# Four resident sums and four turning PSUM banks in place of five and three

## The chip, the cores and the metric

The kernel runs on one core of one Trainium2 chip. The metric is the device time of one execution in microseconds. The kernel before was timed in 3 runs: median 3021.09 us, from 3012.32 to 3032.1 us.

## What is computed

One decoder layer over 1024 tokens of width 1024: a mixing layer (gated linear recurrence and short convolution), then a retrieval layer over 16384 single-neuron experts, then a final norm. Cut to the part that the change touches:

```python
def peer(h, w_query, sub_keys, expert_u, expert_v):
    def block(xb):
        ...                                   # top-k over two lists of 128 keys, 8 heads, 16 picks each
        gate = jax.nn.softmax(best_s, axis=-1)
        u = expert_u[idx]
        v = expert_v[idx]
        act = jax.nn.gelu(jnp.einsum('td,thkd->thk', xb, u).astype(jnp.float32), approximate=False)
        return jnp.einsum('thk,thkd->td', (gate * act).astype(xb.dtype), v)
...
x = x + gate2 * PEER(h)
return rmsnorm(x, final_norm_w)
```

## The kernel before

The 1024 tokens are split. For 672 of them (the dense tokens, columns 0 to 671, in two pieces of 384 and 288 columns, `SPL`) the retrieval is done as two dense matrix products over all 16384 experts, with the gates as a mostly empty matrix. For the other 352 tokens the picked rows of `expert_u` and `expert_v` are fetched by indirect DMA and multiplied on VectorE: this is the background work. It is laid between the dense work by a budget (`along` and `advance`): so many columns of dense products let so many background steps be issued. A background step is one row fetch on GpSimd's queue into one of five row buffers (four named `grow_`, one named `more`, L1084), then either a product with a sum (L1102) or a multiply-add into `gacc` (L1094), both 128x1024 on VectorE.

The last stage, of which the change is a part, runs over 128 blocks of 128 experts. For a block:

- `u_steps` (L1163): the expert rows `uT` times the normed tokens, 24 products of 384 columns into one PSUM bank `pa` and 24 of 288 columns into the next. ScalarE reads each bank with a gelu (L1168). For 40 of the blocks (every third one, as long as they last) this was done in earlier stages, and the result is loaded from DRAM (`ged`).
- `w_step`: times the gates on VectorE (L1384), then a split into a high and a low part: ScalarE copies the high part (L115), VectorE subtracts (L116).
- `v_load`: 128 rows of `expert_v`, split in the same way. The weights `uT` are split so too (`wh`, `wl`).

After every third block `v_phase` (L1403) multiplies three blocks of `v` with the three gated activations. The output has 16 pieces, (j, c): j is one of the two column pieces, c one of 8 groups of 128 features. Each piece takes 9 products here, three blocks by three split terms, into one PSUM bank. From here on a call of `v_phase` is called a v part, and the products of L1163 between two of them a u part. A piece takes one of two ways:

- A fixed piece (listed in `FIXED`) has a PSUM bank of its own (`pacc`), in which all 128 blocks are summed. It is read once, at the end, by ScalarE (L1411).
- Any other piece is a turning piece. It takes a bank from `new_pv` for its 9 products, and VectorE adds it to an accumulator `acc` in SBUF (L1419), which frees the bank. In the first v part this is a copy (L1417), in the last a multiply-add (L1413) on an accumulator that was scaled before (L1487).

PSUM has eight banks: five for the fixed pieces, one `pv`, and two `pa`, which the u parts use as well. `new_pv` deals them in the order `pa`, `pa`, `pv`.

After the last v part each tile of 128 dense tokens is transposed back, with the residual added, into two banks from `new_pv`, and `norm_store` reads these twice (ScalarE L1008, VectorE L1013). The background work, too, takes two banks from `new_pv` for each of its two last groups of tokens (L1120).

Each engine works through its own queue in the order in which a scheduler laid it when the program was built. A wait at the head of a queue holds up all that is behind it.

Of the kernel before, what the change touches and what calls it, by code (L numbers as in the profile page):

```python
# [7 lines left out]
F32 = mybir.dt.float32  # L8
# [11 lines left out]
P = 128  # L20
# [41 lines left out]
WB = 2  # L62
WJ = 0
PAIRS = [(0, 2), (2, 4)]
FIXED = [(0, 1), (0, 4), (0, 7), (1, 2), (1, 5)]
RB = 0.15
RD = 0.0
DG = 2
# [31 lines left out]
def build(tc, A, out, dbg=None):  # L100
# [4 lines left out]
    def pool(st, name, bufs=1, side="left", space=None):  # L105
        kw = {} if space is None else {"space": space}
        if space is DRAM:
            return st.enter_context(tc.tile_pool(name=name, bufs=bufs, **kw))
        if space is PSUM:
            return st.enter_context(tc.tile_pool(name=name, bufs=bufs, reuse_waits="tile", **kw))  # L110
        return st.enter_context(tc.tile_pool(name=name, bufs=bufs, side=side, reuse_waits="tile", **kw))
# [30 lines left out]
    with root:  # L142
# [1200 lines left out]
        while u_early(1.0, "G"):  # L1343
# [6 lines left out]
        psM = pool(stM, "psM", space=PSUM)  # L1350
        accs = {(j, c): mp.tile([P, n], F32, name=f"acc{j}{c}") for j, (_, n) in enumerate(SPL) for c in range(KC)
                if (j, c) not in FIXED}
        fixed = {f: psM.tile([P, 512], F32, name=f"pacc{f[0]}{f[1]}", bufs=1) for f in FIXED}

        turn = [0]

        def new_pv():

            turn[0] = (turn[0] + 1) % 3
            if turn[0]:  # L1360
                return psU.tile([P, 512], F32, name="pa", bufs=2)
            return psM.tile([P, 512], F32, name="pv", bufs=1)

        foldps[0] = new_pv

# [26 lines left out]
        def v_phase(b0, b1):  # L1392
            last = b1 == NK
            for j, (o, n) in enumerate(SPL):
                for c in range(KC):
                    fx = (j, c) in fixed
                    pv = fixed[j, c] if fx else new_pv()
                    i = 0
                    for b in range(b0, b1):
                        wh, wl = Ws[b]  # L1400
                        vh, vl = Vs[b]
                        for l, r in ((vh, wh), (vl, wh), (vh, wl)):
                            T.matmul(pv[:, :n], l[:, c * P:(c + 1) * P], r[:, o:o + n],  # L1403
                                     start=(i == 0 and (not fx or b0 == 0)),
                                     stop=(i == 3 * (b1 - b0) - 1 and (not fx or last)))
                            i += 1
                    if last and fx:
                        accs[j, c] = raw_tile(mp, [P, TD], "W", WS)[:, :n]
                    a = accs.get((j, c))
                    if last and fx:  # L1410
                        C.activation(a, pv[:, :n], AF.Copy, scale=modc[:, 5, c:c + 1])  # L1411
                    elif last:
                        V.scalar_tensor_tensor(a, pv[:, :n], modc[:, 5, c:c + 1], a, op0=OP.mult, op1=OP.add)  # L1413
                    elif fx:
                        pass
                    elif b0 == 0:
                        V.tensor_copy(a, pv[:, :n])  # L1417
                    else:
                        V.tensor_tensor(a, a, pv[:, :n], op=OP.add)  # L1419
                    if not last:  # L1420
                        along(3.0 * (b1 - b0) * n)
                if last:
                    for t in range(o // P, -(-(o + n) // P)):
                        w = WT[t]
                        parts = []
                        for q in range(2):
                            pt = new_pv()[:w]
                            for c in range(4):
                                cs_ = slice((q * 4 + c) * P, (q * 4 + c + 1) * P)
                                d = pt[:, c * P:(c + 1) * P]  # L1430
                                if j:
                                    T.matmul(d, ident[:w, :w], x1s[t][:w, cs_], start=True, stop=False)
                                    T.matmul(d, accs[j, q * 4 + c][:, t * P - o:t * P - o + w], ident, start=False, stop=True)
                                else:
                                    T.transpose(d, accs[j, q * 4 + c][:, t * P - o:t * P - o + w], ident)
                            if j == 0:
                                sl = slice(q * 512, (q + 1) * 512)
                                V.tensor_tensor(rs[t][:w, sl], pt, x1s[t][:w, sl], op=OP.add)
                                pt = rs[t][:w, sl]
                            parts.append(pt)  # L1440
                        norm_store(mp, REST + t * P, w, parts, fw, rs[t], sq)
# [99 lines left out]
```

## Time and profile before

| | us |
|---|---|
| median of 3 runs | 3021.09 |
| the profiled execution, its own time | 3030.79 |
| its span | 3029.0 |
| PE busy | 2864.4 (95%) |
| DVE busy | 2528.4 (83%) |
| ACT busy | 941.1 (31%) |
| POOL busy | 890.8 (29%) |

PE is TensorE's products, DVE is VectorE, ACT is ScalarE, POOL is GpSimd, SP is the queue that issues the plain DMAs. A busy share is over the whole span. The granted clock is TensorE's, as a share of full speed; its mean over the span is 0.975. The last stage runs from 1265 us to the end. A wait is the idle time of an engine just before an instruction, with the work that ended it named after the arrow. The chain of waits is followed back from the last instruction.

### The profile page before, as it was taken

To read this page: it belongs to the slowest core of one execution; us is meant where nothing else is said; L and a number is where in the kernel's file an instruction comes from. 1 tells how busy PE (TensorE), PEld (TensorE's weight loads), DVE (VectorE), ACT (ScalarE), POOL (GpSimd) and SP (SyncE) were. 2 spreads that over 40 slices of the span, in tenths; PEclk is the share of its full clock that TensorE was granted. 3 is DMA by queue.
4 is the path that set the end of the run, shared out by engine and by line. 5 is a ranking of instruction groups with operands and counts; after the bars stand their busy time and mean duration, and the time that the engine had idled before them with its cause. 6 is when DMAs were issued, how large, how long until landed. Compare 5 with 4: busy or idle time off the path is not lost.

```text
span 3029.0 us, 47154 instructions
## 1 busy us (share of the span) xinstructions
PE 2864.4 (95%) x18190; PEld 2696.5 (89%) x18190; DVE 2528.4 (83%) x5325; ACT 941.1 (31%) x1549; POOL 890.8 (29%) x726
## 2 busy tenths in 40 slices
PE   8999999989999999998999999989999999999998
PEld 6887888869989889998989999889999999989897
DVE  7885559978999978488888989888898888789887
ACT  5644655333222545322221222211222222122222
POOL 0000000000000000055555554445555545455451
PEclk9999999989999999999999999999999999999999
DMA  8324342243123877788989899889898998889894
GB/s 283 128 90 152 129 139 70 84 148 136 62 91 117 253 237 237 248 306 305 329 314 318 319 328 339 309 307 324 306 350 319 331 326 311 312 314 326 297 320 157
DMA packets 288675, 740.00 MB, mean 244 GB/s; under 512 B 27873, under 2 KB 122081, under 8 KB 282050
## 3 DMA queue, kind: packets, MB, share of 16 engines
q0 software_dynamic: 102944, 374.78, 35.2%
q1 hardware_dynamic: 185506, 362.22, 34.8%
q8 instruction: 142, 2.33, 0.3%
q14 instruction: 83, 0.68, 0.1%
HBM read 666.29 MB, written 70.52 MB: 243 GB/s over the span
## 4 chain that ended last, share of the span: by engine, by line
PE 29%; DVE 28%; DMA 22%; issue 12%; POOL 5%; ACT 3%; SPq 0%; DVEq 0%; POOLq 0%; ACTq 0%
PE pa L1163 11%; DMA wl<-in_uT 5%; PE pp L469 5%; DMA Wl<-ged 4%; DVE gacc L1094 4%; DVE wl L116 3%; PE pa L1403 2%; PE pg L1330 2%; PE pp L875 2%; DVE acc L1419 2%; DVE vl L116 2%; DMA more<-in_v,idx 1%; DVE Wl L1384 1%; DVE s L926 1%; PE pacc L1403 1%
## 5 line engine op out<-in xcount | busy, mean ns | idle before, releaser
L1163 PE MATMUL pa<-h2h,wh 128*128 128x384 f32 (+1 forms) x1840 | 597.4, 325 | 42.0 <-DVE acc L1419 38.4
L1163 PE MATMUL pa<-h2l,wh 128*128 128x384 f32 (+1 forms) x1840 | 593.6, 323 | 0.0
L1163 PE MATMUL pa<-h2h,wl 128*128 128x384 f32 (+1 forms) x1840 | 589.9, 321 | 2.6 <-DVE wl L116 2.6
L1163 PEld LDWEIGHTS pa<-h2h,wh 128*128 128x128 f32 x1840 | 352.7, 192 | 51.5 <-DVE acc L1419 45.0
L1163 PEld LDWEIGHTS pa<-h2h,wl 128*128 128x128 f32 x1840 | 353.8, 192 | 2.9 <-DVE wl L116 2.9
L1163 PEld LDWEIGHTS pa<-h2l,wh 128*128 128x128 f32 x1840 | 354.1, 192 | 0.0
L1403 PE MATMUL pa<-Wh,vh 128*128 128x288 f32 (+1 forms) x941 | 303.3, 322 | 39.6 <-ACT Wl L1168 25.5
L115 ACT ACTIVATE Wh<-Wl 128x672 fp32r<-128x672 f32 x128 | 98.1, 767 | 768.9 <-PE pa L1403 393.6
L115 ACT ACTIVATE wh<-wl 128x1024 fp32r<-128x1024 f32 x187 | 197.8, 1058 | 385.9 <-DMA wl<-in_uT 180.2
L1403 PE MATMUL pa<-Wh,vl 128*128 128x288 f32 (+1 forms) x941 | 298.4, 317 | 0.0
L1403 PE MATMUL pa<-Wl,vh 128*128 128x288 f32 (+1 forms) x941 | 297.8, 316 | 0.0
L116 DVE TENSOR_TENSOR wl<-wl,wh 128x1024 fp32r<-128x1024 f32 x187 | 228.8, 1224 | 82.1 <-ACT wh L115 80.5
L1403 PEld LDWEIGHTS pa<-Wh,vh 128*128 128x128 f32 x941 | 179.0, 190 | 53.2 <-ACT Wl L1168 32.4
L1403 PE MATMUL pacc<-Wh,vh 128*128 128x384 f32 (+1 forms) x640 | 206.0, 323 | 1.3 <-ACT vh L115 1.3
L1403 PE MATMUL pacc<-Wh,vl 128*128 128x384 f32 (+1 forms) x640 | 206.2, 322 | 0.5 <-DVE vl L116 0.5
L1403 PE MATMUL pacc<-Wl,vh 128*128 128x384 f32 (+1 forms) x640 | 205.8, 322 | 0.0
L1403 PEld LDWEIGHTS pa<-Wl,vh 128*128 128x128 f32 x941 | 179.3, 191 | 0.4 <-DVE Wl L116 0.3
L1403 PEld LDWEIGHTS pa<-Wh,vl 128*128 128x128 f32 x941 | 179.3, 191 | 0.0
L116 DVE TENSOR_TENSOR vl<-vl,vh 128x1024 fp32r<-128x1024 f32 x128 | 156.5, 1222 | 15.1 <-ACT vh L115 12.9
L115 ACT ACTIVATE vh<-vl 128x1024 fp32r<-128x1024 f32 x128 | 134.4, 1050 | 99.4 <-DMA vl<-in_v 50.9
L1403 PE MATMUL pv<-Wh,vh 128*128 128x288 f32 (+1 forms) x467 | 149.2, 319 | 14.9 <-DVE acc L1419 13.4
L469 PE MATMUL pp<-h1h,wh 128*128 128x512 f32 x384 | 156.7, 408 | 0.0
(1940 smaller groups left out, 7342.6 us busy)
## 6 DMA issues: line engine op xcount, KB each, us to landing
wl<-in_uT SPq DMA_DIRECT2D x128, 512.0 KB
vl<-in_v SPq DMA_DIRECT2D x128, 512.0 KB
gd<-stg SPq DMA_DIRECT2D x21, 2048.0 KB
gsb<-gd SPq DMA_DIRECT2D x32, 1344.0 KB
wl<-in_win SPq DMA_DIRECT2D x48, 512.0 KB
wa<-in_wada SPq DMA_DIRECT2D x16, 1024.0 KB
wl<-in_wq SPq DMA_DIRECT2D x32, 512.0 KB
ged<-ge SPq DMA_DIRECT2D x40, 336.0 KB
```

The costliest lines, as they stand in the source:

```text
L115: C.activation(hi, src, AF.Copy)
L116: V.tensor_tensor(lo, src, hi.bitcast(F32), op=OP.subtract)
L469: T.matmul(pp, l[:, k], r[k], start=(i == 0), stop=(i == 3 * KC - 1))
L875: T.matmul(pq[:, :m], l[:, k], hs[k, r][:, o:o + m], start=(i == 0), stop=(i == 3 * KC - 1))
L926: V.match_replace(s2, tsv[:, 0:8], vals, NEG)
L1094: V.scalar_tensor_tensor(ac, r, aw[:, j:j + 1], ac, op0=OP.mult, op1=OP.add))
L1163: T.matmul(pa[:, :n], l[:, k], h2[k, r][:, o:o + n], start=(i == 0), stop=(i == 3 * KC - 1))
L1330: T.matmul(pg[:, e_], Ps[r][:, e // 2, :, e % 2], O1[:, e // 2, :, e % 2], start=(r == 0), stop=(r == 1))
L1384: V.tensor_tensor(gv, gv, gs[b // GB][:, :, b % GB], op=OP.mult)
L1403: T.matmul(pv[:, :n], l[:, c * P:(c + 1) * P], r[:, o:o + n], start=(i == 0 and (not fx or b0 == 0)), stop=(i == 3 * (b1 - b0) - 1 and (no ...
L1419: V.tensor_tensor(a, a, pv[:, :n], op=OP.add)
```

## The change

One of the five fixed pieces becomes a turning piece, the four that stay fixed are chosen anew, and the PSUM bank that comes free becomes a second `pv`. `new_pv` now deals `pa`, `pv`, `pa`, `pv`. A v part then has 12 turning pieces and 4 fixed ones in place of 11 and 5. Between two fixed pieces there are now three turning ones, before there were two. The number of products is the same.

```diff
@@ -62,7 +62,7 @@
 PAIRS = [(0, 2), (2, 4)]
-FIXED = [(0, 1), (0, 4), (0, 7), (1, 2), (1, 5)]
+FIXED = [(0, 1), (0, 5), (1, 1), (1, 5)]
 RB = 0.15
@@ -1356,10 +1356,10 @@
         def new_pv():
 
-            turn[0] = (turn[0] + 1) % 3
+            turn[0] ^= 1
             if turn[0]:
                 return psU.tile([P, 512], F32, name="pa", bufs=2)
-            return psM.tile([P, 512], F32, name="pv", bufs=1)
+            return psM.tile([P, 512], F32, name="pv", bufs=2)
```

The order of the instructions moves with it. First VectorE, in the second half of one v part in the middle of the stage (`acc_...` is the accumulator of one turning piece, the name behind it the bank it is read from; `more` and `grow_` are row buffers). Before:

```order
L1419 TENSOR_TENSOR acc_13120<-acc_13120,pv 128x288
L1094 SCALAR_TENSOR_TENSOR gacc<-more,aw,gacc 128x1024
L1419 TENSOR_TENSOR acc_13121<-acc_13121,pa 128x288
L1102 SCALAR_TENSOR_TENSOR grow__21422,aw<-grow__21422,hx 128x1024
L1419 TENSOR_TENSOR acc_13122<-acc_13122,pa 128x288
L1419 TENSOR_TENSOR acc_13123<-acc_13123,pv 128x288
L1094 SCALAR_TENSOR_TENSOR gacc<-grow__21447,aw,gacc 128x1024
L1102 SCALAR_TENSOR_TENSOR more,aw<-more,hx 128x1024
L1419 TENSOR_TENSOR acc_13124<-acc_13124,pa 128x288
L1102 SCALAR_TENSOR_TENSOR grow__21470,aw<-grow__21470,hx 128x1024
L1419 TENSOR_TENSOR acc_13125<-acc_13125,pa 128x288
```

and now, at the same place:

```order
L1419 TENSOR_TENSOR acc_13121<-acc_13121,pa 128x288
L1094 SCALAR_TENSOR_TENSOR gacc<-more,aw,gacc 128x1024
L1419 TENSOR_TENSOR acc_13122<-acc_13122,pv 128x288
L1102 SCALAR_TENSOR_TENSOR grow__21466,aw<-grow__21466,hx 128x1024
L1419 TENSOR_TENSOR acc_13123<-acc_13123,pa 128x288
L1419 TENSOR_TENSOR acc_13124<-acc_13124,pv 128x288
L1094 SCALAR_TENSOR_TENSOR gacc<-grow__21491,aw,gacc 128x1024
L1102 SCALAR_TENSOR_TENSOR more,aw<-more,hx 128x1024
L1419 TENSOR_TENSOR acc_13125<-acc_13125,pa 128x288
L1102 SCALAR_TENSOR_TENSOR grow__21514,aw<-grow__21514,hx 128x1024
L1419 TENSOR_TENSOR acc_13126<-acc_13126,pv 128x288
```

The background steps between the evictions stand as before; the banks now alternate, and this half ends on a `pv` where it ended on two `pa`. Over the stage L1419 stands 492 times on VectorE, 451 times before. On TensorE 28 of the 42 v parts that follow a full u part began with a `pa` bank, and now all 42 do; ten ended on two `pa`, and now each of the 42 ends on a `pv`. The orders of SP and of POOL stay, but for three weight loads and one row fetch that move by a place or two.

Second, ScalarE in a u part (`wh` is the high part of the weights of a later block, `Wl<-pa` the gelu). Before:

```order
L1168 ACTIVATE Wl<-pa 128x384
L115 ACTIVATE vh<-vl 128x1024
L115 ACTIVATE wh<-wl 128x1024
L1168 ACTIVATE Wl<-pa 128x288
L115 ACTIVATE Wh<-Wl 128x672
```

and now:

```order
L1168 ACTIVATE Wl<-pa 128x384
L115 ACTIVATE vh<-vl 128x1024
L1168 ACTIVATE Wl<-pa 128x288
L115 ACTIVATE wh<-wl 128x1024
L115 ACTIVATE Wh<-Wl 128x672
```

The gelu of the second bank has moved ahead of the weight split, here and at some other places of the stage.

Third, ScalarE at the end of the program, where `norm_store` squares the last three tiles of dense tokens, each out of two banks. Before:

```order
L1008 ACTIVATE vh,sf<-pa 128x512 x2
L1008 ACTIVATE vh,sf<-pv 128x512
L1008 ACTIVATE vh,sf<-pa 128x512
L1008 ACTIVATE vh,sf<-pa 32x512
L1008 ACTIVATE vh,sf<-pv 32x512
```

and now:

```order
L1008 ACTIVATE vh,sf<-pa 128x512
L1008 ACTIVATE vh,sf<-pv 128x512
L1008 ACTIVATE vh,sf<-pa 128x512
L1008 ACTIVATE vh,sf<-pv 128x512
L1008 ACTIVATE vh,sf<-pa 32x512
L1008 ACTIVATE vh,sf<-pv 32x512
```

Each tile now has a `pa` and a `pv`, and two tiles have all four banks between them.

## Rows read from the trace of the kernel before

**Rows 1.** Busy time by engine: last stage, then tail; PE, PEld, DVE, ACT, POOL, clock, DMA.
```profile
1265.00:2985.00 1720.00, 1622.33 (x10187) 1594.68 (x10186) 1488.97 (x2065) 383.00 (x539) 876.23 (x698) 0.98 0.89 316
2985.00:3029.00 44.00, 32.57 (x214) 26.34 (x212) 28.68 (x97) 11.89 (x31) 0.00 (x0) 0.86 0.24 90
```
**Rows 2.** The page's chain of waits, whole span, by engine.
```profile
PE 29%; DVE 28%; DMA 22%; issue 12%; POOL 5%; ACT 3%; SPq 0%; DVEq 0%; POOLq 0%; ACTq 0%
```
**Rows 3.** Waits of PE, 1265 to 2985: us in total, times, longest us.
```profile
PE pa L1163 <- DVE acc L1419: 38.4, 19, 6.7
PE pa L1403 <- ACT Wl L1168: 25.5, 19, 3.0
PE pa L1403 <- DVE acc L1419: 13.7, 17, 2.2
PE pv L1403 <- DVE acc L1419: 13.4, 10, 3.4
```
**Rows 4.** Waits of DVE, the same stretch and columns.
```profile
DVE wl L116 <- ACT wh L115: 21.1, 17, 2.3
DVE Wl L1384 <- ACT Wl L1168: 17.5, 15, 2.2
DVE more L1102 <- DMA more<-in_u,idx: 16.4, 7, 6.9
```
**Rows 5.** Line 1419, the same stretch: instructions (ns min/median/max); DVE's idle before them.
```profile
L1419 DVE TENSOR_TENSOR acc<-acc,pa x301: 440/456/559, 1318.0 to 2975.0; 128x288 f32<-128x288 f32 x82, 128x384 f32<-128x384 f32 x69
L1419 DVE TENSOR_TENSOR acc<-acc,pv x150: 441/455/558, 1314.5 to 2972.1; 128x288 f32<-128x288 f32 x82, 128x384 f32<-128x384 f32 x68
...
  PE pa L1403: 6.1, 12
  PE pv L1403: 3.6, 6
```
**Rows 6.** Timeline of PE, two waits: start us, us, instruction [idle before <-releaser].
```profile
2106.71 0.61 PE L1403 MATMUL pa<-Wh,vh 128*128 128x288 f32 x1 [1.25 <-DVE acc L1419]
...
2157.87 0.69 PE L1163 MATMUL pa<-h2h,wh 128*128 128x384 f32 x1 [6.67 <-DVE acc L1419]
```
**Rows 7.** Timeline of PE, neighbours without a wait, of either width.
```profile
2000.09 0.29 PE L1163 MATMUL pa<-h2h,wl 128*128 128x288 f32 x1
2000.22 0.29 PE L1163 MATMUL pa<-h2h,wh 128*128 128x288 f32 x1
...
2004.94 0.33 PE L1403 MATMUL pacc<-Wh,vl 128*128 128x384 f32 x1
2005.11 0.34 PE L1403 MATMUL pacc<-Wl,vh 128*128 128x384 f32 x1
```
**Rows 8.** Busy time as in Rows 1, in three stretches behind eviction waits.
```profile
1340.30:1344.30 4.00, 3.96 (x18) 3.96 (x19) 4.00 (x5) 0.00 (x0) 2.14 (x2) 0.59 0.82 264
2158.00:2163.50 5.50, 5.50 (x18) 5.50 (x19) 5.46 (x7) 0.00 (x0) 2.34 (x3) 0.50 0.76 235
2591.50:2597.00 5.50, 5.50 (x24) 5.50 (x24) 4.88 (x10) 0.23 (x1) 3.22 (x4) 0.50 0.84 275
```
**Rows 9.** Timeline of PE, first and last wait for a gelu.
```profile
1393.40 0.45 PE L1403 MATMUL pa<-Wh,vh 128*128 128x384 f32 x1 [2.95 <-ACT Wl L1168]
...
2816.95 0.45 PE L1403 MATMUL pa<-Wh,vh 128*128 128x384 f32 x1 [2.36 <-ACT Wl L1168]
```
**Rows 10.** Pieces of the chain in order of time: start us, us, what.
```profile
1899.26 4.96 DMA grow__19282<-in_u,idx
...
1907.51 9.10 PE pa L1163 x47
```
**Rows 11.** Timeline of PE in the tail.
```profile
3011.37 0.49 PE L1432 MATMUL pa<-wl,ident 128*128 128x128 f32 x2 [1.88 <-DVE hx L1013]
...
3017.07 0.63 PE L1432 MATMUL pv<-vl,ident 32*32 32x128 f32 x2 [0.99 <-DVE gacc L1013]
...
3021.01 0.64 PE L1433 MATMUL pv<-ident,acc 128*32 128x128 f32 x2
```

## The prediction

> **What bounds the kernel now.** I read the busy times of the stage first, then TensorE's waits in it, then the chain of waits, then the tail. The last stage takes 1720 of the 3029 us; TensorE is busy for 1622 us of it, VectorE for 1489 (87%), and the DMA engines for 0.89 of it [rows 1]. So three resources are close to full, and TensorE leads by a little. Nothing ahead of the stage changes, nor does the number of products.
>
> TensorE's waits in the stage have two causes [rows 3]. For a bank that VectorE has still to empty it waits 38.4 us before u parts (19 times) and 13.7 + 13.4 us inside v parts (27 times): 65.5 us in 46 waits. For a gelu on ScalarE it waits 25.5 us. No transfer is in the list, so the data are there in time and the banks are not. A wait costs more than its idle time: in the 5.5 us behind the longest one, 6.67 us [rows 6], the granted clock was 0.50, which is the lower of its two levels, 1.2 GHz, and so or nearly so it stood in 14 such stretches of 3 to 6 us, of which the first, the longest and the last are shown [rows 8]; 13 of the 14 stand behind an eviction wait.
>
> Why is VectorE late? Of the 451 evictions only 18 found it waiting for TensorE, 9.7 us in all [rows 5]. The other 433 were behind in its queue, among background steps, and one of these can itself stand for a fetched row, up to 6.9 us [rows 4]. The chain of waits says the same: TensorE has 29% of it, VectorE, DMA and POOL together 55% [rows 2]. A typical crossing: a fetch of 4.96 us, the VectorE work behind it, an eviction, and only then 9.10 us of TensorE [rows 10]. **So the eviction wait is where two loops meet**: TensorE's products, and the loop of VectorE, row buffer and fetch. A fourth bank loosens the joint. It makes neither loop shorter, and the second gets longer by the extra evictions.
>
> **The change, part by part.** Durations are from the profiled execution, 3030.8 us with its ends; that is 9.7 us above the median of the runs, so I take the difference over to the median, 3021.1.
>
> *Banks.* A product of 384 columns steps on after 0.17 us, one of 288 after 0.13 [rows 7], so a piece of 9 takes 1.57 or 1.17 us. Between two uses of a bank there now stands one turning piece more. Each of the 27 waits inside v parts shrinks by at least 1.17 us; they have 1.0 us on average, at most 3.4, and I leave 6 of 27.1 us. Before a u part more changes. Ten v parts ended on two `pa`, so the next u part wanted a bank that had been filled only two pieces earlier; now the end is always a `pv`, and the first bank the u part wants was filled five pieces earlier, one of them fixed. That is 3.5 us more cover there and 1.2 us or so elsewhere. Of 38.4 us I leave 12, most of it in the two longest waits. **Together 65.5 becomes 18: 47 us less idle.** Bounds: nothing, if VectorE falls behind as much as the banks give, and 65.5.
>
> *Clock.* The mean of 0.98 over 1720 us bounds what the lower clock costs at 34 us [rows 1]; a stretch of 4.0 us at 0.59 or of 5.5 us at 0.50 loses 1.6 to 2.7 us [rows 8], so 13 of them cost 23 or so. With two thirds of the waits gone I take two thirds: **15 us**, between 0 and 23.
>
> *Gelu.* Every v part now starts on a `pa`, the bank of the u part's 384 columns, so it always needs that gelu at once; 28 of 42 did before. Waits for a gelu are 25.5 us, 0.9 us for each of the 28, and 14 more heads make 13 us. Against this, the order puts the second gelu ahead of the weight split at some places, where it stood behind a split that waits for its load. I take **10 us more**, between 5 and 41 (14 times the longest but a little, 2.95 us [rows 9]).
>
> *Evictions.* L1419 stands 492 times for 451: 41 more, at 0.456 us by the median [rows 5], is **19 us of VectorE**; at most 0.559 each, 23. POOL and SP issue the same work in all but the same order, so the fetches are unchanged in number. What is queued behind an eviction is a background step, and behind that the row buffer that POOL waits for. The removed fixed piece saves one read on ScalarE at the very end and gives VectorE one there, half a microsecond either way.
>
> *Tail.* The last three tiles take two banks each. With three banks the second half of the second tile waits 1.88 us for the norm of the tile before it, and the last half of the third waits 0.99 us, after which its pairs of products take 0.63 us until 3021.7 [rows 11]. With four banks each tile finds two free ones. The end hangs on this chain. The 2.9 us of waits go, and some of the slow half with them: **4 us**, between 2 and 5.
>
> *What of it reaches the end.* TensorE is ahead by 47 + 15 - 10 = 52 us. The other loop gains only where VectorE stood idle for TensorE's products: through the two splits and gate steps 21.1 + 17.5 us [rows 4], at the evictions 9.7 [rows 5], 48 us as a cap. Idle time for fetched rows is not helped: the same rows must come in a shorter stage through DMA engines that are already at 0.89. I take half of 52, **26 us**, since the chain gives the two sides about equal parts of what is not TensorE's own. Of the 19 us of evictions I let two thirds, 13 us, through, the part of the chain that is not TensorE's. Sum: -26 + 13 - 4 = -17, that is 3014 us for the profiled execution and **3004 us** against the median.
>
> **The rivals.**
>
> *TensorE alone sets the pace* (25%). For it: it is the busiest engine, and no wait of it names a transfer. Against it: its 29% of the chain. Then all 52 us pass, the evictions fit in VectorE's idle 13%, and with the tail 56 us go: 2965 us.
>
> *The wait only changes its name* (15%). VectorE is behind at 433 of 451 evictions; it may fall behind by one more bank and stand as late as before. Then nothing comes from the banks, the evictions cost 19 us and the gelu 10, the tail gives 4: 3046 us. The Trainium skill, page "TensorE: Matmul & The Clock Gate", section "HAM oscillation — how this bites in real kernels", tells of a kernel in which double buffering of PSUM gave no further gain once TensorE was kept busy. By that rule the bank and clock terms would be zero here and the time this rival's; the 46 waits for banks in this trace speak against carrying it over whole.
>
> *The head of the v part becomes the wait* (10%), and the kernel is slower. Every v part starts on the bank of the gelu that was issued last but one, with only the 3.1 us of the 288-column products as cover (24 at 0.13). If ScalarE, held by splits that wait for VectorE, ends that gelu later than this in the 14 v parts that used to start elsewhere, each pays up to 2.95 us and a slow stretch of 1.6 or so: 64 us against the 30 us that the forecast wins from banks and tail, with 13 for evictions: 3068 us at the worst, 3060 for a likely case. Against it: the 28 heads that start so already pay 0.9 us on average.
>
> That the banks are not dealt by turns can be left out: the order shows it.
>
> **The numbers.** Forecast 50%: 3004, by itself from 2985 to 3025, which is half or twice the share that I let through. One per cent, 30 us, is about what can be told from no change. Faster than 2991: the 25% of the second case and 7% of the forecast's own spread, 32%. Slower than 3051: the 10% of the last and 2% of the third, 12%. The rest, 56%, is within 1%. The range from 2952 to 3042 takes in the bounds of the bank term below, where 56 us may be 69 with all waits gone, and above most of the third case; it leaves out about 2 in 10.
>
> **What would show it.** Eviction waits of TensorE at or under 20 us, none of them at the start of a u part behind two `pa`; gelu waits near 35 us, now at the heads of nearly all v parts; a granted clock of 0.99 in the stage; no bank wait in the tail; VectorE's idle time behind ScalarE's splits shorter, its waits for fetched rows longer. If the eviction waits are gone and the stage still takes 1720 us, the loop of VectorE and fetches is the bound, and my share of one half was too high. If waits for rows do not grow, the share was too low. If TensorE's eviction waits stay at 60 us, the lateness of VectorE grew with the cover and the third case holds.

## The result and the profile after

The changed kernel takes 2998.78 us (median of 7 runs, 2986.61 to 3004.09) against 3021.09 (median of 7 by now, 3012.32 to 3032.1): ratio 0.9919 [0.9894, 0.9944], 22 us or 0.8% less. The forecast was 3004, within 1%. So the time came out nearly as forecast; whether the reasons hold is what the experiments asked, and several of them do not.

The two profiled executions are 44 us apart (3030.79 and 2986.61 us), twice as far as the medians: the one before lies 10 us above its median, the one after is the fastest of its seven. So a second profile of the changed kernel was taken (called "again" below, 3004.25 us), and where a count matters both are given.

Busy time of the changed kernel in the last stage and its tail, columns as in [rows 1]:

```profile
1265.00:2940.00 1675.00, 1601.89 (x10150) 1579.71 (x10151) 1502.15 (x2096) 379.80 (x534) 847.95 (x698) 0.99 0.90 324
2940.00:2985.00 45.00, 37.22 (x252) 31.34 (x250) 34.72 (x111) 13.51 (x35) 0.00 (x0) 0.94 0.28 101
```

The stage is 45 us shorter, with the same 698 spans on POOL and 31 more instructions on VectorE. VectorE is now busy for 90% of it (1502 of 1675) in place of 87%, and the clock is at 0.99 in place of 0.98. Cut into pieces of 2 us, the stage before lost 38 us to the lower clock (the sum of each piece's length times what its granted clock lacked to 1), the stage after 19 us, and again 26 us.

TensorE's waits of the changed kernel in the stage, columns as in [rows 3]:

```profile
PE pa L1403 <- ACT Wl L1168: 41.7, 34, 3.0
PE pa L1163 <- DVE acc L1419: 12.0, 4, 6.1
PE pa L1403 <- DVE acc L1419: 11.6, 11, 2.4
PE pv L1403 <- DVE acc L1419: 4.9, 9, 1.5
```

The eviction waits (the last three) are down from 65.5 us in 46 to 28.5 us in 24; most of it left the heads of the u parts. The gelu waits (the first) are up from 25.5 to 41.7 us, and 52.7 again. Together, by the sums in the table below: from 92 us to 70, and 77 again. The gelu waits do not all stand at the head of a v part: in the timeline after, 30.5 us in 24 of them do, and 11.2 us in 10 stand at its fourth piece, where the second `pa` is wanted.

The timeline of TensorE after, at the longest wait left, and the busy time behind it, columns as in [rows 6] and [rows 8]:

```profile
2134.73 0.61 PE L1163 MATMUL pa<-h2h,wh 128*128 128x288 f32 x1 [6.08 <-DVE acc L1419]
```

```profile
2135.00:2140.50 5.50, 5.50 (x25) 5.50 (x26) 5.46 (x7) 0.00 (x0) 2.35 (x3) 0.53 0.64 190
```

Four banks did not remove this: a u part still waited 6.08 us for an eviction, and the clock behind it stood at 0.53 for 5.5 us, as it did before [rows 6, 8].

Waits of VectorE after, columns as in [rows 4], and line 1419 as in [rows 5]:

```profile
DVE Wl L1384 <- ACT Wl L1168: 17.6, 12, 2.8
DVE wl L116 <- ACT wh L115: 14.4, 11, 2.7
DVE more L1102 <- DMA more<-in_u,idx: 12.3, 5, 6.3
```

```profile
L1419 DVE TENSOR_TENSOR acc<-acc,pa x246: 436/494/551, 1314.9 to 2936.6; 128x384 f32<-128x384 f32 x82, 128x288 f32<-128x288 f32 x41
L1419 DVE TENSOR_TENSOR acc<-acc,pv x246: 435/496/555, 1318.4 to 2937.9; 128x384 f32<-128x384 f32 x82, 128x288 f32<-128x288 f32 x41
...
  PE pv L1403: 2.1, 5
  PE pa L1403: 1.1, 2
```

There are 492 evictions for 451, and only 7 of them found VectorE waiting for TensorE, 18 before: VectorE is behind more often than it was. Of its waits behind ScalarE the one at the split is shorter, 14.4 us for 21.1, and the one at the gate step unchanged, 17.6 for 17.5 [rows 4]. All its waits for fetched rows from 1268 to 2900 us, added over the rows of the view (one for each buffer), went from 130 us to 102, and 99 again. So the loop of VectorE and fetches gained as well. (Most of this total lies in rows of a single wait each, which are not shown.)

The end of TensorE's work in the tail, columns as in [rows 11], from the first product that transposes one of the last tiles (L1432), before and then after:

```profile
3003.86 0.49 PE L1432 MATMUL pa<-wh,ident 128*128 128x128 f32 x2 [0.81 <-DVE acc L1413]
```

```profile
2964.50 0.49 PE L1432 MATMUL pa<-wh,ident 128*128 128x128 f32 x2
...
2971.62 0.39 PE L1433 MATMUL pv<-ident,acc 128*128 128x128 f32 x2
2972.10 0.40 PE L1432 MATMUL pa<-vl,ident 32*32 32x128 f32 x2
...
2977.09 0.41 PE L1433 MATMUL pv<-ident,acc 128*32 128x128 f32 x2
```

No wait is left here, and the last pairs take 0.41 us where they took 0.64. From the start of that first product to the end of the span it is 25.1 us before, 20.3 after and 21.9 again.

The page's chain of waits after, which answers to [rows 2], and its longest piece in order of time:

```profile
issue 27%; DVE 25%; DMA 20%; PE 20%; POOL 5%; ACT 2%; SPq 0%; DVEq 0%; POOLq 0%; ACTq 0%
```

```profile
843.66 443.12 issue
```

"issue" has 27% where it had 12, PE 20% where it had 29. But 443 us of it are one piece, nearly all ahead of the last stage (1265 us), where nothing was changed and where this profile shows no releaser (the longest such piece before is 15.5 us). Shares of the whole span do not tell the stages apart.

### The profile page after: what moved, and what is told of

It is laid out like the page before. It is cut to its first block, busy times and chain, and to the rows that moved or that the text cites. A ratio compares the mean times of both kernels' runs of the same rounds, so it can differ in the third digit from the quotient of the medians.

```text
span 2984.8 us, 47174 instructions
## 1 busy us (share of the span) xinstructions
PE 2850.0 (95%) x18190; PEld 2687.0 (90%) x18190; DVE 2547.3 (85%) x5369; ACT 939.3 (31%) x1548; POOL 862.6 (29%) x726
## 4 chain that ended last, share of the span: by engine, by line
issue 27%; DVE 25%; DMA 20%; PE 20%; POOL 5%; ACT 2%; SPq 0%; DVEq 0%; POOLq 0%; ACTq 0%
PE pp L469 5%; DVE gacc L1094 5%; DMA wl<-in_uT 3%; DVE wl L116 3%; DVE acc L1419 3%; DMA Wl<-ged 2%; PE pq L875 2%; PE pp L875 2%; DVE vl L116 2%; DVE Wl L1384 1%; DMA more<-in_u,idx 1%; PE pa L1163 1%; PE ps L579 1%; PE pp L380 1%; POOL more L1084 1%
## 5 line engine op out<-in xcount | busy, mean ns | idle before, releaser
L1403 PE MATMUL pa<-Wh,vh 128*128 128x384 f32 (+1 forms) x768 | 251.5, 327 | 53.6 <-ACT Wl L1168 41.7
L1403 PE MATMUL pv<-Wh,vh 128*128 128x384 f32 (+1 forms) x768 | 245.4, 320 | 5.2 <-DVE acc L1419 4.9
L1403 PE MATMUL pa<-Wl,vh 128*128 128x384 f32 (+1 forms) x768 | 245.8, 320 | 0.7 <-DVE Wl L116 0.7
L1403 PE MATMUL pa<-Wh,vl 128*128 128x384 f32 (+1 forms) x768 | 245.6, 320 | 0.0
L1403 PE MATMUL pv<-Wh,vl 128*128 128x384 f32 (+1 forms) x768 | 243.7, 317 | 0.0
L1403 PE MATMUL pv<-Wl,vh 128*128 128x384 f32 (+1 forms) x768 | 243.3, 317 | 0.0
L1403 PEld LDWEIGHTS pa<-Wh,vh 128*128 128x128 f32 x768 | 145.7, 190 | 67.7 <-ACT Wl L1168 52.1
L1403 PE MATMUL pacc<-Wh,vh 128*128 128x384 f32 (+1 forms) x512 | 163.6, 320 | 1.5 <-ACT vh L115 1.5
L1403 PE MATMUL pacc<-Wh,vl 128*128 128x384 f32 (+1 forms) x512 | 163.7, 320 | 0.6 <-DVE vl L116 0.6
L1403 PE MATMUL pacc<-Wl,vh 128*128 128x384 f32 (+1 forms) x512 | 163.0, 318 | 0.0
```

## The experiments

The theories, with the numbers that the expectations use. 1: the eviction wait is where the loops meet, and the fourth bank loosens it (the prediction's). 2: VectorE alone is the bound. 3: it matters that no v part ends on two `pa`. 4: the waits for fetched rows carry the gain. 5: the even places of the fixed pieces carry it. 6: the pattern does, which is even, the same in each v part, and does not end on a `pa`; the bank and the number of evictions are worth nothing in the stage. "Even" stands here for a fixed piece at the same place in every group of four. The five old places are evenly spaced too, one in three, and that order does not gain.

A pattern is written in the order in which TensorE does the 16 pieces: a is a `pa`, v is a `pv`, F is a fixed piece. It is read from the timeline. Before, three patterns follow one another, since 11 is not a multiple of three: the one in the table, `aFvaFavF aaFvaFav` and `aFavFaaF vaFavFaa`. In the other kernels, but for the one before with six rows, one pattern returns in each v part.

| kernel | pattern | median us | ratio to before [95%] | eviction waits | gelu waits | row waits | slow clock | tail |
|---|---|---|---|---|---|---|---|---|
| before | `vFaaFvaF avFaaFva` and two more | 3021.09 | 1 | 66.1 | 25.8 | 130 | 38 | 25.1 |
| after | `aFvavFav aFvavFav` | 2998.78 | 0.9919 [0.9894, 0.9944] | 28.5 | 41.7 | 102 | 19 | 20.3 |
| again | the same | 2995.83 | 0.9919 [0.9893, 0.9944] | 24.3 | 52.7 | 99 | 26 | 21.9 |
| e1, three banks | `aFav aFav aFav aFav` | 2995.38 | 0.9917 [0.9891, 0.9944] | 25.3 | 46.7 | 93 | 17 | 25.9 |
| e2, one unread | `aFvavFav aFvavFav` | 2995.39 | 0.9918 [0.9891, 0.9945] | 30.7 | 38.2 | 112 | 24 | 21.9 |
| e4, end on pv | `aFvaFavF aaFvaFav` | 3015.83 | 0.9974 [0.9953, 0.9995] | 53.7 | 30.5 | 130 | 24 | 25.1 |
| f, old places | `aFavFaaF vaFavaav` | 3016.96 | 0.9983 [0.9962, 1.0003] | 39.2 | 34.2 | 102 | 29 | 24.6 |
| e3, pv first | `vFavaFva vFavaFva` | 3010.43 | 0.9955 [0.9937, 0.9974] | 73.4 | 4.2 | 106 | 33 | 20.3 |
| g, five even | `aFavaFav aFavaFaF` | 2979.7 | 0.9842 [0.9822, 0.9862] | 17.3 | 46.2 | 98 | 17 | 24.5 |
| h, fixed last | `avaFvavF avaFvavF` | 2987.02 | 0.9871 [0.9845, 0.9898] | 1.9 | 66.9 | 109 | 32 | 20.4 |
| r, before with six rows | as before | 2993.27 | 0.9909 [0.9884, 0.9934] | 58.8 | 9.4 | 86 | 39 | 26.6 |
| r, after with six rows | as after | 2955.51 | 0.9763 [0.9733, 0.9792] | 33.2 | 22.5 | 53 | 21 | 20.4 |
| e1 with six rows | as e1 | 2970.97 | 0.9815 [0.9795, 0.9835] | 27.4 | 21.3 | 41 | 20 | 26.4 |
| g with six rows | as g | 2964.5 | 0.9794 [0.9774, 0.9815] | 42.2 | 11.2 | 49 | 21 | 24.8 |

The last five columns are us of one profiled execution each: TensorE's waits for evictions and for gelus and VectorE's for fetched rows, added over the rows of the view of waits from 1268 us on (the latter to 2900), what the stage loses to the lower clock, worked out as above, and the length of the tail from the first product of L1432. The views of single kernels below end at 2900 us, so their sums can be a microsecond or so lower. Each ratio is against runs of the kernel before on the same chip, so a median is not to be set beside another of other chips to the last us; again, e1, e2 and e4 ran on one chip, f, e3 and the two r on another, g and the other two of six rows on a third, h on a fourth.

**Again.** No edit.

> The changed kernel once more, as the measure for the runs beside it. Every theory: 0.81% below the kernel before, 2997 us where that takes 3021; eviction waits of TensorE in the last stage near 28 us, gelu waits near 42.

The ratio is the same to four digits. The eviction waits are 24 us, the gelu waits 11 us more than in the first profile.

**e1: the fourth bank taken away, all else as changed.**

```diff
-            turn[0] ^= 1
+            turn[0] = (turn[0] + 1) % 3
...
-            return psM.tile([P, 512], F32, name="pv", bufs=2)
+            return psM.tile([P, 512], F32, name="pv", bufs=1)
```

> The change without its fourth bank: four fixed pieces and 12 turning ones, dealt over pa, pa, pv; one PSUM bank lies unused. Theory 1 (eviction waits are the joint, the fourth bank loosens it): eviction waits back at 50 us or more, and 41 more evictions to pay, 3025 us, 1% above the changed kernel. Theory 2 (VectorE alone is the bound, the bank is worth nothing): as the changed kernel, within 5 us. Theory 3 (what counts is that no v part ends on two pa, which this kernel keeps): 3005 us, close to the changed kernel.

Waits of TensorE in the stage in e1:

```profile
PE pa L1403 <- ACT Wl L1168: 46.7, 30, 4.7
PE pa L1403 <- DVE acc L1419: 14.6, 13, 3.1
PE pa L1163 <- DVE acc L1419: 5.3, 3, 2.0
PE pv L1403 <- DVE acc L1419: 4.2, 10, 2.0
```

With three banks the eviction waits are as low as with four (25 us), and so is the time (0.9917 against 0.9919). **The fourth bank is not what shortened the stage.** Where did its cover go? By the timelines an eviction starts some time after the end of its piece's last product: on average 2.5 us before (37 v parts of 11 turning pieces), 3.4 us after (41 of 12; again 3.6), and 2.4 us in e1. VectorE's order is all but the same in e1 and after (some 20 of 2200 instructions stand elsewhere), so in this order VectorE falls behind by about what the bank allows. This is no rule: in h, which has four banks and another order, it is 2.2 us, and in e4, which has three, 3.1. In the tail the bank does count. TensorE's timeline there in e1:

```profile
2980.48 0.49 PE L1432 MATMUL pa<-wl,ident 128*128 128x128 f32 x2 [1.88 <-DVE hx L1013]
2987.36 0.40 PE L1432 MATMUL pa<-vl,ident 32*32 32x128 f32 x2 [0.61 <-DVE gacc L1013]
```

Both waits of [rows 11] are back, and the tail takes 25.9 us. What e1 loses there, 4 to 5.5 us, is too little to be seen in its ratio.

**e2: one eviction less in each v part.**

```diff
-                    else:
+                    elif (j, c) != (0, 4):
```

> The changed kernel with one eviction less in each v part but the first and the last: the sum of piece (0, 4) is formed in its bank and not added up, so VectorE has 11 evictions, as before, with four banks. That piece of the output is left out. Theory 1, with two thirds of an eviction's 0.46 us on the path: 13 us less than the changed kernel, 2985 us. Theory 2: the full 19 to 20 us less, 2978 us. If TensorE alone sets the pace: no change, 2998 us.

To the end of the last v part (2970 us here, 2981 again) VectorE is busy for 1502 us where it was for 1522 again, and the time does not move: 2995.39 and 2995.83 us on one chip. An eviction more or less in each v part, some 20 us of VectorE, is not felt within what these runs can tell (each ratio has an interval of 0.0027, 8 us, to either side). Theory 2 falls.

**e4: the kernel before, each v part started on the same bank, so that it ends on `pv`.**

```diff
+            turn[0] = 1
```

> The kernel before with five fixed pieces and three banks, only that the dealing starts anew in each v part so that every one begins on pa and ends on pv. Theory 1: the waits before u parts fall from 38 us to 20, those inside v parts stay at 27, gelu waits grow by 10; 3015 us, within 0.4% of the kernel before. Theory 2: 3021 us. Theory 3: it brings all of the gain without a bank, 2998 us.

Waits of TensorE in the stage in e4:

```profile
PE pa L1404 <- ACT Wl L1168: 28.2, 28, 4.5
PE pa L1404 <- DVE acc L1420: 21.8, 24, 3.1
PE pa L1163 <- DVE acc L1420: 17.3, 9, 5.7
PE pv L1404 <- DVE acc L1420: 14.6, 14, 3.6
```

The waits at the heads of u parts fall from 38.4 to 17.3 us, which is most of what theory 3 asked, but the ones inside the v parts rise from 27.1 to 36.4, and the time falls by a quarter of a per cent. Theory 3 alone does not make the gain.

**f: four fixed pieces and three banks, at four of the five old places.** It differs from e1 in this alone.

```diff
-FIXED = [(0, 1), (0, 5), (1, 1), (1, 5)]
+FIXED = [(0, 1), (0, 4), (0, 7), (1, 2)]
```

> Four fixed pieces of the five old ones, (0, 1), (0, 4), (0, 7), (1, 2), with three banks: 12 turning pieces, but unevenly placed, two between fixed ones first and seven in a row at the end. Theory 5 (even places): the evictions at the end of the v part run late, eviction waits back at 60 us or more, 3020 us or slower. Theory 4: only the number counts, one step more of VectorE in the v part gives the rows time; row waits near 100 us and 2998 us.

Waits of TensorE in the stage in f:

```profile
PE pa L1403 <- ACT Wl L1168: 34.2, 25, 4.2
PE pa L1163 <- DVE acc L1419: 15.2, 8, 4.2
PE pv L1403 <- DVE acc L1419: 13.4, 10, 2.9
PE pa L1403 <- DVE acc L1419: 9.4, 10, 2.3
```

Same banks, same number of evictions, other places: 0.9983 [0.9962, 1.0003] against e1's 0.9917 [0.9891, 0.9944]. The places are worth 0.7%, which is most of the change's gain. (Five of f's turning pieces are 384 columns wide and six of e1's, which is 4 us of VectorE in f's favour.) The eviction waits differ by 14 us and the slow clock by 12; the gelu waits give 12 of it back.

f has five turning pieces in a row at the end, `avaav` (the expectation says seven). On three banks the last two of them, and the u part behind them, want a bank that was filled only three pieces earlier, with two pieces, 2.3 us by [rows 7], between; in e1 three pieces stand between, one of them fixed, 3.5 us. There the waits are: by the timeline 12.5 of f's 39 us stand at these two pieces, where e1 has none, and 15 us at the heads of u parts, where e1 has 5. VectorE is no later in f than in e1 (2.1 us behind the piece's end, and 2.4).

**e3: the changed kernel with its banks dealt from `pv` on, so that a v part ends on `pa`.**

```diff
-        turn = [0]
+        turn = [1]
```

> The changed kernel with the dealing begun one step later, so that each v part starts on pv and ends on pa. The first pa is then wanted 3.1 us after the u part. Gelu waits of TensorE fall from 42 to 15 us; eviction waits before u parts grow from 12 to 20. If TensorE's waits are what the end hangs on: 15 us less, 2982 us. If VectorE and the fetches set the pace: the waits come back as eviction waits, 2997 us.

Waits of TensorE in the stage in e3:

```profile
PE pa L1163 <- DVE acc L1419: 52.0, 23, 7.9
PE pv L1403 <- DVE acc L1419: 14.3, 10, 3.0
...
PE pa L1403 <- ACT Wl L1168: 4.2, 6, 2.2
```

No v part wants the gelu's bank first, and the gelu waits are 4.2 us. But the last piece leaves a `pa` full, and 52 us of waits stand at the heads of u parts. Half of the gain is gone (the intervals, [0.9937, 0.9974] and [0.9894, 0.9944], just overlap). So an end on `pa` does cost waits, and four banks do not cover it.

**g: five fixed pieces and three banks as before, four of the pieces one in each group of four, the last one at the end.**

```diff
-FIXED = [(0, 1), (0, 4), (0, 7), (1, 2), (1, 5)]
+FIXED = [(0, 1), (0, 5), (1, 1), (1, 5), (1, 7)]
...
+            turn[0] = 0
```

> The kernel before with its five fixed pieces, three banks and 11 evictions, only placed otherwise: (0, 1), (0, 5), (1, 1), (1, 5), (1, 7), and the dealing begun anew in each v part, so that each one is pa F pa pv four times with the last pv fixed. Theory 6 (the gain of the change is the even pattern that is the same in every v part and does not end on a pa; bank and number of evictions are worth nothing in the stage): row waits of VectorE near 100 us, eviction waits of TensorE 25 to 35 us, 3000 us, 0.7% below the kernel before; the 4 us of the tail are missing. Theory 1 as far as it stands (a twelfth turning piece and a fourth bank are needed): 3015 us or more, as the kernel that only ends on pv.

Waits of TensorE in the stage in g:

```profile
PE pa L1404 <- ACT Wl L1168: 46.2, 33, 3.3
PE pa L1404 <- DVE acc L1420: 11.5, 8, 2.5
PE pv L1404 <- DVE acc L1420: 4.3, 6, 2.7
PE pa L1163 <- DVE acc L1420: 1.5, 1, 1.5
```

The kernel before, with its fixed pieces moved and the dealing begun anew in each v part, gains 1.6%, twice what the change gains, without the fourth bank and without the 41 evictions. The u parts wait 1.5 us for evictions where they waited 38.4. Two things are changed here at once; a dealing begun anew alone, from another bank, is e4, which gains a quarter of a per cent.

**h: the changed kernel with its four fixed pieces at the ends of the groups of four.**

```diff
-FIXED = [(0, 1), (0, 5), (1, 1), (1, 5)]
+FIXED = [(0, 3), (0, 7), (1, 3), (1, 7)]
```

> The changed kernel, four banks and four fixed pieces, with the fixed ones moved to the end of each group of four: (0, 3), (0, 7), (1, 3), (1, 7), so that every v part ends on a fixed piece, as the kernel with five evenly placed ones does that took 0.984 of the time before. If the fixed piece in the last place is what that kernel has over the changed one: eviction waits before u parts fall from 12 to under 5 us, and the ratio is 0.984 or less, 2977 us. If it is the eviction less: 0.992, as the changed kernel, 2998 us.

Waits of TensorE in the stage in h:

```profile
PE pa L1403 <- ACT Wl L1168: 64.6, 44, 3.5
PE pa L1163 <- ACT Wl L1168: 2.3, 3, 1.4
...
PE pa L1403 <- DVE acc L1419: 0.8, 1, 0.8
```

The eviction waits are gone (1.9 us in 3), and the gelu waits are 66.9 us in 47. Their sum, 69 us, is that of the changed kernel, 70. This is the plainest case of a wait that changes its name. By the timeline 21.6 us of the gelu waits, in 19, stand at the heads of v parts, and 42.9 us, in 25, at the third piece: it is the second `pa`, which this order wants one piece sooner than `aFva` does, and it waits for the gelu of the 288 columns. One of them, the last product ahead of it, and the clock behind it:

```profile
1672.43 0.34 PE L1403 MATMUL pv<-Wl,vh 128*128 128x384 f32 x1
1674.72 0.44 PE L1403 MATMUL pa<-Wh,vh 128*128 128x384 f32 x1 [1.95 <-ACT Wl L1168]
```

```profile
1676.00:1679.00 3.00, 3.00 (x11) 3.00 (x10) 3.00 (x5) 0.77 (x1) 0.67 (x1) 0.50 0.94 344
```

e1 and g want their second `pa` third as well, and most of their gelu waits stand there (33.7 and 42.8 us). The time of h still falls, to 0.9871 [0.9845, 0.9898]; the interval touches the change's at 0.9894 to 0.9898, so to have the fixed pieces at the ends of the groups is likely, but not surely, worth half a per cent. All four moved, so this does not tell the last one from the others. Between h and g there is left 0.3%, less than the intervals, for one eviction per v part, one bank and what else differs in their patterns.

**r: a sixth row buffer, in the kernel before and in the changed one.** The room comes from another pool.

```diff
+        sixth = []
...
-                    r = grow(n) if taken_rows[0] % (ROWS + 1) else gp.tile([P, DM], F32, name="more", bufs=1)[:n]
+                    k = taken_rows[0] % (ROWS + 1 + len(sixth))
+                    r = (grow(n) if 0 < k <= ROWS else
+                         (sixth[0] if k else gp).tile([P, DM], F32, name="more", bufs=1)[:n])
...
+        sixth.append(mp)
```

> The kernel before with a sixth row buffer in the last stage (128x1024, in SBUF), nothing else. Theory 4 (VectorE's waits for fetched rows, 131 us in the stage before and 93 to 113 in the kernels that gain, carry the gain): the waits fall to 100 us or less and TensorE's eviction waits with them, 2995 us. Theory 5 (the place of the fixed pieces among the 16 carries it, whatever rows do): row waits fall, but the time stays within 5 us of the kernel before, 3018 us. A side effect against both: more fetches in flight at 0.89 of the DMA engines, each later, no change at all.

> The changed kernel with the same sixth row buffer. Theory 4: the row waits of 100 us fall to 70, and the time by 10 to 20 us to 2980; the distance to the kernel before with six buffers shrinks to half or less. Theory 5: the distance stays 24 us, both moving alike.

Waits of TensorE in the stage, the kernel before with six rows, then the changed one with six:

```profile
PE pa L1407 <- DVE acc L1423: 28.5, 12, 7.0
PE pa L1166 <- DVE acc L1423: 25.8, 13, 5.5
PE pa L1407 <- ACT Wl L1171: 9.4, 8, 2.9
```

```profile
PE pa L1407 <- ACT Wl L1171: 21.4, 23, 2.6
PE pa L1166 <- DVE acc L1423: 19.9, 6, 6.5
PE pa L1407 <- DVE acc L1423: 10.9, 7, 3.2
```

The buffer alone gives 0.9909, as much as the change. VectorE's row waits fall from 130 to 86 us, and TensorE's two kinds of waits from 92 to 68 us, without a hand laid on banks or pieces. Both together give 0.9763 [0.9733, 0.9792], more than the product of the two, 0.983, though by hardly more than the intervals. **This is the fastest kernel here**: 2955.51 us, faster than both. (Its profile is that of its slowest run, 2969.94 us.)

**e1 and g with six rows.** The same lines as in r, added to e1 and to g.

> Four even fixed pieces, three banks, one bank unused, and the sixth row buffer in the last stage. Theory 1 in the form that the bank counts once rows come early: the changed kernel with six buffers took 2955 us, this one lacks the bank and takes 2975 us or more. Theory 6: the bank is worth its 4 us in the tail and no more, 2960 us.

> Five fixed pieces evenly placed, three banks, and the sixth row buffer: the pattern and the buffer without the bank and without the twelfth eviction. Theory 6: 2960 us, with the changed kernel that has six buffers. If the eviction left out counts now that the rows come early: 2945 us. Theory 1: 2985 us or more.

With six rows the fourth bank is worth something: 0.9815 [0.9795, 0.9835] without it, 0.9763 [0.9733, 0.9792] with it, though the intervals barely part and the two ran on different chips. Of the 15 us some 6 lie in the tail (26.4 and 20.4 us). The traces do not show the rest: the two profiled executions are 1.5 us apart (2971.41 and 2969.94), and TensorE's two kinds of waits sum to 49 us without the bank and 56 with it. The Trainium skill, page "TensorE: Matmul & The Clock Gate", section "HAM oscillation — how this bites in real kernels", tells of a kernel in which double buffering of PSUM gave no more once TensorE was kept busy. In the stage with five rows e1 agrees with that; with six rows the times of these two runs speak, weakly, against it. And g, which was ahead with five rows, is not with six (0.9794): its eviction waits rise from 17 to 42 us while its gelu waits fall from 46 to 11.

## Why the prediction was right, and where it was not

**Banks: the size was near, the cause was wrong.** The step said 65.5 us become 18, since a fourth bank and an end on `pv` give cover. The waits became 24 to 28 us, but e1 has 25 without the bank. This is the step that failed: it priced the change by the distance between two uses of a bank and took VectorE's lateness as given. In this order the lateness grew with the cover, by 0.9 to 1.1 us (e1 has none of that), as the third case said. What shortened the waits is the other half of the same edit, the places of the fixed pieces, which the prediction used only for the ends of the v parts. f against e1 shows it with the same banks and the same number of evictions, and g, with the dealing begun anew, shows it without a bank. The distance between two uses does count, but it is the places that set it (f). It is not all: in e4 the `pa` behind `FaaFv` has three pieces between its uses, as in e1, and 15 of the 36 us inside e4's v parts stand there; there VectorE is later (3.1 us over all pieces, against 2.4).

**Clock: right in its number, in part by luck.** Forecast 15 us, measured 12 to 19 (38 to 26 or 19). The prediction bounded the loss before at 34 us, with a mean clock that was rounded to 0.98, and priced it at 23 or so; it was 38, and a third to a half of it went, where two thirds were taken. The slow stretches go with the waits, of either kind: in h, which has next to no eviction waits, each of the 15 stands beside a gelu wait, and the loss is 32 us.

**Gelu: too small, and read at the wrong place.** Forecast +10 us, between 5 and 41; measured +16 and +27. The prediction laid the 25.5 us on 28 heads of v parts, 0.9 us each. By the timeline only 10.1 us, in 6 waits, stand at a head before, 0.4 us for each of the 28; 15.4 us, in 13, stand at the third or fourth piece, where the second `pa` is wanted. One of these, two pieces behind a head:

```profile
1521.70 0.52 PE L1403 MATMUL pa<-Wh,vh 128*128 128x384 f32 x1 [2.47 <-ACT Wl L1168]
```

After, the heads have 30.5 us and again 36.2, which is 0.7 and 0.9 us for each of 42. So the price of a head about doubled, and that 0.9 was near is luck. Why it doubled is not shown. That TensorE arrives sooner when it waits less elsewhere does not explain it alone: e1 waits as little for evictions and has 12.9 us at its heads, h has next to no eviction waits and 21.6 us.

**Evictions: wrong.** 13 us were let through; e2 shows none that can be told from zero. VectorE has room for the 19 us: from 1268 to 2940 us it is idle for 227 us before and for 173 after, 191 again.

**Tail: right.** Forecast 4 us; 4.8 in the one profile and 3.2 in the other, and e1 has both waits and 25.9 us again.

**What reaches the end: the half is not borne out.** TensorE does the same products before and after, so its waits, its slow clock and the tail are nearly the whole account. From before to after they give 22 + 19 + 5 = 46 us, where the profiled times differ by 44; from before to again 15 + 12 + 3 = 30, where they differ by 27. Nothing is halved on the way. These are waits as they came out, so what came back under another name is in them already; the prediction halved once more, after it had taken the gelu waits off. (It is no exact account: e1 gives 40 us by it against 30 measured, h 33 against 42, e4 21 against 8.) The prediction's 52 us were too many, since the gelu waits took back more; the half and the 13 us of evictions brought it down again. The two errors cancelled, and the forecast's 3004 us is near for that reason. Without them the sum would have been 56 us, the first rival's 2965.

**The other loop gained, and the prediction said that it would not.** It had "its waits for fetched rows longer"; they went from 130 to 102 and 99 us. By the prediction's own test the share was then too low. The row waits fall in all kernels with four fixed pieces or an even pattern, and stay at 130 in e4. They fall in f as well, to 102 us, and f does not gain, so shorter row waits alone do not carry the gain (theory 4).

**The rivals.** TensorE alone: its end, 2965 us, did not come, but its account is the one that adds up. The wait that changes its name: half true, banks to gelus, with no loss. The head of the v part: there, at 30 to 36 us, and the kernel is not slower.

**What stays open.** Why VectorE waits longer for rows before and in e4 (130 us) than in e1 (93 us), and is later at its evictions in e4, is not known; both have one eviction less in each v part than e1. A long run of turning pieces is not the reason: f has the longest, and its row waits are 102 us. No run separates the places of the fixed pieces from those at which the background steps are laid. Nor is it known why f, with row waits of 102 us and waits of TensorE of 73 us in its profile, takes as long as e4; its profile is one of its fastest runs (3008.19 against a median of 3016.96).

## What to carry to other kernels

A wait for a bank names the engine that empties it, but that engine may fall behind by as much as it is given, as here in one order of the pieces and not in another (h): after adding a buffer, take it away from the finished change and see whether the time moves. When several resources are close to full, price the sum of all the waits of the in-order engine and ask which wait is met sooner when another goes; a wait that moves is no gain. A change that frees a buffer and reorders work in one edit is two changes; try the order alone, which here was worth twice the whole (g), and look for the loop on the other side, which was worth as much (the sixth row buffer).

## What was not expected of the chip

41 more instructions of about half a microsecond on an engine that is busy for 90% of the stage cost nothing that can be measured. A PSUM bank that was worth nothing in the whole time (0.9917 and 0.9919) came to be worth about 0.5% when another resource was relieved (0.9815 and 0.9763, with intervals that barely part). And the time lost to the lower clock does not follow the sum of the waits: 19 us beside 70 us of waits after, 32 us beside 69 in h.
